# Gate loads moved from SyncE's queue to ScalarE's, value tiles held back, 86 expert tiles ahead instead of 92

## The chip, the cores and the metric

One core of a Trainium2 chip runs the whole program. The metric is the device time of one execution in microseconds; before the change the median of three runs is 1597.53 us (1596.8 to 1598.02). The engines are named as in the profile: PE (matrix multiply), PEld (its weight loads), DVE (vector), ACT (scalar), POOL (GpSimd, which issues the gathers) and SP (SyncE, which here only issues DMAs). ACT issues DMAs too, in line with its own arithmetic.

## The reference

One decoder layer on 512 tokens of width 1024. A first half (a gated mixer, a sparse attention, an output projection) makes h. The second half, where the change lies, adds a product-key expert layer with 16384 one-row experts:

```
q   = rmsnorm(h) @ wq                      # 8 heads, 2 halves of 128
sub = q . subkeys                          # 128 keys a half
pick the 16 best of each half, then the 16 best pairs (i, j) a head
expert = i * 128 + j ;  gate = softmax(best)
a = gelu(x . u_tab[expert]) ;  y = sum gate * a * v_tab[expert]
```

## The kernel before

The first 384 of the 512 tokens take the expert layer densely, the last 128 sparsely by gathering rows.

Dense part. The 16384 experts are 128 tiles of 128 experts. For each tile j, `expert_in(j)` loads the tile of `u_tab` (512 KB, `load_w`, tile `wraw`, three buffers), splits it into a rounded high part (`whi`, ACT, L89) and a low part (`wlo`, DVE, L90), multiplies it with the 384 tokens in 24 matmuls (`pa` in PSUM, two buffers) and takes the result out through a gelu on ACT. Tiles 0 to 39 stay in SBUF. Tiles from 40 up to `AHEAD` are written out by ACT's queue: gelu into `actd` (two buffers, L669) and the spill store `ad<-actd` (L670). These tiles "run ahead": they need no gates. Tiles from `AHEAD` on are made later.

Gates. While the tiles run ahead, the routing code picks experts, and one-hot matmuls (`pg`, L865) build a dense gate matrix. ACT copies it from PSUM into `ch` (L867) and stores it to DRAM as 24 chunks of 1 MB (`gd<-ch`, L869). The numbering here is "1st" to "24th" chunk.

Last stage. For each tile j from 0 to 127: `load_v` loads a value tile (`vraw`, 512 KB, four buffers, split like an expert tile), `load_g` loads the gates of eight tiles at once (`gg`, 1.5 MB in pieces of 512 bytes, two buffers, L904; the first of them in two parts, since chunk 24 is made last), the product of activation, gate and its split (`pr`, `ph`, `pl`) are formed, and 18 matmuls add to `y`. Here the remaining expert tiles and the reads of spilled tiles (`st<-ad`, L921) are mixed in. The sparse part (gathers by POOL, `gt`, dot products and sums on DVE) runs beside all of it.

What sets the order. A scheduler places the instructions of each engine when the program is built; each engine then runs its list strictly in that order. An instruction that waits holds everything behind it on its engine, DMA issues included. The expert loads, value loads, gate loads and reads of spilled tiles are all in SP's list. `tc.issue_after(x)` tells the scheduler to place what it covers behind x. The names used below: expert tile 68 ends in `pa_8208`, 69 in `pa_8242`, 70 in `pa_8279`, 71 in `pa_8313`, 72 in `pa_8350`, 73 in `pa_8384`, 74 in `pa_8421`, 75 in `pa_8455`, 76 in `pa_8492`.

## Time and profile before

| what | value |
|---|---|
| median of three runs | 1597.53 us (1596.8 to 1598.02) |
| the profiled execution, its own time | 1590.94 us |
| its span (first to last instruction) | 1589.2 us |
| PE busy | 1550.9 us, 98% |
| DVE busy | 1265.7 us, 80% |
| ACT busy | 656.9 us, 41% |
| moved by DMA | 387.13 MB, mean 244 GB/s |

The span is first to last instruction; the rest of the execution's time is 1.7 us. PE is "busy" nearly throughout, so time can only come from the places where it is not: the 40 slices of the page show one, slices 21 and 22 (795 to 874 us), where the PE row drops to 6 and 8 while DMA reads 9 and 9. That is the place where the tiles that run ahead meet the start of the last stage. From there to the end DMA is at 8 or 9 of ten in nearly every slice.

### The profile page before, as it was taken

The numbers are of one execution on the slowest core, as the hardware profiler recorded it, in microseconds if no ns is written. First come the engines' busy times: TensorE is split into PE (matmuls) and PEld (weight loads), VectorE is DVE, ScalarE is ACT, GpSimd is POOL, SyncE is SP. The second block draws the span as 40 slices with busy tenths as digits, with TensorE's granted clock in tenths as the row PEclk, the third lists the DMA queues.
The fourth block names the chain that finished last, engine by engine and source line by source line (L and its number), as shares of the span: only waits on it lengthen the run. The fifth ranks groups of instructions, "written<-read, shape, count | busy, mean of one in ns | idle before, by whom it ended". The sixth has DMA issues, their size and how long they took to land.

```text
span 1589.2 us, 22526 instructions
## 1 busy us (share of the span) xinstructions
PE 1550.9 (98%) x8173; PEld 1354.3 (85%) x8173; DVE 1265.7 (80%) x2648; ACT 656.9 (41%) x976; POOL 359.8 (23%) x280
## 2 busy tenths in 40 slices
PE   8998999999999999999968999999999999999998
PEld 6777777888899999999968988888888888888887
DVE  5599945557999999999846688778888878887885
ACT  5453453322335456676713333333333333333332
POOL 0010000000001251111223343333333334344330
PEclk9999999999999999999989999999999999999999
DMA  6211225253213255899899999999999999999983
GB/s 219 80 53 67 93 71 194 93 224 134 80 67 129 84 199 189 294 326 325 318 342 330 349 329 339 340 339 346 347 344 339 347 337 339 337 328 318 323 319 113
DMA packets 154655, 387.13 MB, mean 244 GB/s; under 512 B 12336, under 2 KB 74800, under 8 KB 150960
## 3 DMA queue, kind: packets, MB, share of 16 engines
q1 hardware_dynamic: 106736, 216.07, 38.4%
q0 software_dynamic: 36864, 134.23, 23.8%
q10 hardware_dynamic: 10944, 35.39, 6.0%
q8 instruction: 64, 1.05, 0.3%
q14 instruction: 47, 0.39, 0.1%
HBM read 346.59 MB, written 39.06 MB: 243 GB/s over the span
## 4 chain that ended last, share of the span: by engine, by line
PE 75%; issue 9%; DVE 7%; DMA 7%; POOL 2%; ACT 1%; SPq 0%; POOLq 0%; DVEq 0%; ACTq 0%
PE y L95 9%; PE y L96 9%; PE y L94 9%; PE pa L94 6%; PE pa L95 6%; PE pa L96 6%; DMA gt<-in_v_rows,eid 4%; PE pcol L95 2%; PE pcol L94 2%; PE pcol L96 2%; POOL gt L678 2%; PE pq L94 2%; PE pq L95 2%; PE pq L96 2%; DVE wlo L90 2%
## 5 line engine op out<-in xcount | busy, mean ns | idle before, releaser
L94 PE MATMUL pa<-hh,whi 128*128 128x384 f32 (+2 forms) x1040 | 351.4, 338 | 18.6 <-ACT actd L669 17.7
L95 PE MATMUL pa<-hl,whi 128*128 128x384 f32 (+2 forms) x1040 | 350.7, 337 | 0.0
L96 PE MATMUL pa<-hh,wlo 128*128 128x384 f32 (+2 forms) x1040 | 350.7, 337 | 0.0
L678 POOL DMA_INDIRECT gt<-in_u_rows,eid x128 | 184.4, 1440 | 596.1 <-DVE dots L691 407.3
L95 PE MATMUL y<-wlo,ph 128*128 128x512 f32 x768 | 299.6, 390 | 2.9 <-DVE wlo L90 2.9
L96 PE MATMUL y<-whi,pl 128*128 128x512 f32 x768 | 299.5, 390 | 0.0
L94 PE MATMUL y<-whi,ph 128*128 128x512 f32 x768 | 298.1, 389 | 0.0
L89 ACT CAST whi<-wraw 128x1024 fp32r<-128x1024 f32 x179 | 188.1, 1053 | 243.6 <-PE pa L95 94.4
L90 DVE TENSOR_TENSOR wlo<-wraw,whi 128x1024 fp32r<-128x1024 f32 x179 | 218.2, 1221 | 81.5 <-ACT whi L89 79.4
L678 POOL DMA_INDIRECT gt<-in_v_rows,eid x128 | 163.1, 1274 | 259.7 <-DVE h2l L701 215.8
L94 PEld LDWEIGHTS pa<-hh,whi 128*128 128x128 f32 x1040 | 196.7, 189 | 21.4 <-ACT actd L669 18.6
L934 ACT CAST ph<-pr 128x384 fp32r<-128x384 f32 x128 | 66.0, 516 | 332.4 <-PE y L95 292.6
L95 PEld LDWEIGHTS pa<-hl,whi 128*128 128x128 f32 x1040 | 196.8, 189 | 1.5
L96 PEld LDWEIGHTS pa<-hh,wlo 128*128 128x128 f32 x1040 | 196.6, 189 | 0.4 <-DVE wlo L90 0.4
L701 DVE SCALAR_TENSOR_TENSOR h2l<-gt,coef,h2l 128x1024 f32<-128x1024 f32 x128 | 163.9, 1281 | 36.1 <-DMA gt<-in_v_rows,eid 35.6
L89 ACT CAST whi<-vraw 128x1024 fp32r<-128x1024 f32 x128 | 134.3, 1049 | 107.3 <-PE pa L95 55.2
L691 DVE CUSTOM_DVE_ANT_0 gt<-gt,hn 128x1024 f32<-128x1024 f32 x128 | 155.6, 1220 | 27.1 <-DMA gt<-in_u_rows,eid 25.5
L95 PEld LDWEIGHTS y<-wlo,ph 128*128 128x128 f32 x768 | 144.1, 188 | 33.1 <-DVE wlo L90 3.7
L90 DVE TENSOR_TENSOR wlo<-vraw,whi 128x1024 fp32r<-128x1024 f32 x128 | 156.2, 1220 | 18.1 <-ACT whi L89 17.3
L96 PEld LDWEIGHTS y<-whi,pl 128*128 128x128 f32 x768 | 144.1, 188 | 29.9
L94 PEld LDWEIGHTS y<-whi,ph 128*128 128x128 f32 x768 | 144.2, 188 | 29.1
L867 ACT ACTIVATE ch<-pg 128x512 f32<-128x512 f32 x96 | 97.0, 1108 | 52.5 <-PE pg L865 47.9
(307 smaller groups left out, 2105.9 us busy)
## 6 DMA issues: line engine op xcount, KB each, us to landing
vraw<-in_v_rows SPq DMA_DIRECT2D x128, 512.0 KB
wraw<-in_ut SPq DMA_DIRECT2D x115, 512.0 KB
gd<-ch ACTq DMA_DIRECT2D x24, 1024.0 KB
gg<-gd SPq DMA_DIRECT2D x15, 1536.0 KB
wraw<-in_wcol SPq DMA_DIRECT2D x20, 512.0 KB
ad<-actd ACTq DMA_DIRECT2D x52, 192.0 KB
st<-ad SPq DMA_DIRECT2D x52, 192.0 KB
wraw<-in_wq SPq DMA_DIRECT2D x16, 512.0 KB
```

The source lines that it names most:

```text
L89: A.copy(hi, raw)
L90: V.tensor_tensor(lo, raw, hi.bitcast(F32), ALU.subtract)
L94: T.matmul(ps, lh, rh, start=start, stop=False)
L95: T.matmul(ps, lh, rl, start=False, stop=False)
L96: return T.matmul(ps, ll, rh, start=False, stop=stop)
L678: G.indirect_dma_start(out=t, out_offset=None, in_=table, in_offset=bass.IndirectOffsetOnAxis(ap=eid[:, s:s + 1], axis=0))
L691: V.tensor_tensor_reduce(out=t, in0=t, in1=hn3, scale=1.0, scalar=0.0, op0=ALU.mult, op1=ALU.add, accum_out=dots[:, s:s + 1])
L701: V.scalar_tensor_tensor(h2l, t, coef[:, s:s + 1], h2l, ALU.mult, ALU.add)
L867: A.activation(ch[:, :, to + t4:to + t4 + 4].rearrange("p i t -> p t i"), pg, AF.Copy, scale=1.0 / GS)
L934: A.copy(ph, pr)
```

## The change

`load_g` issues the gate loads on ACT's queue in place of SP's. The gate loads inside the loop are placed behind the last `ph` copy made so far (`hi_copy`) in place of the value load of tile j. `load_w` keeps its load instructions in a list, and value tiles from the third on are placed behind the load of the last expert tile that runs ahead. `AHEAD` is 86, so six expert tiles (86 to 91) move into the last stage, with six spill stores and six reads fewer.

```
--- before.py
+++ after.py
@@ -78,9 +78,11 @@
     TK = 12
     NW = 8
 
+    loads = []
+
     def load_w(src, wp=wp, raws=RAW):
         raw = wp.tile([P, D], F32, name="wraw", tag="wraw", bufs=raws)
-        SY.dma_start(raw, src)
+        loads.append(SY.dma_start(raw, src))
         return split_w(raw, wp)
 
     def split_w(raw, wp=wp):
@@ -636,7 +638,7 @@
     TO = 8
     NCH = ND // TC
     JG = 8
-    AHEAD = 92
+    AHEAD = 86
     KEPT = 40
     EARLY = 2
     GS = 2.0 ** 15
@@ -654,7 +656,7 @@
     stash = ctx.enter_context(tc.tile_pool(name="stash", bufs=1, reuse_waits="tile"))
     big = [stash.tile([P, 3, ND], F32, name=f"st{i}") for i in range((KEPT - 1) // 3)]
     free = [t[:, a, :] for t in big for a in range(3)]
-    pre = {}
+    pre, uload = {}, [None] * len(acts)
     for i, t in enumerate(big):
         pre[len(acts) + 3 * i] = t.rearrange("p a t -> p (a t)")[:, :D]
         SY.dma_start(pre[len(acts) + 3 * i], ut[len(acts) + 3 * i])
@@ -662,6 +664,7 @@
     def expert_in(j):
 
         hi, lo = split_w(pre[j]) if j in pre else load_w(ut[j])
+        uload.append(loads[-1])
         ps = psa.tile([P, S], F32, name="pa", tag="pa")
         expert_mm(ps, hi, lo, 0, ND)
         if KEPT <= j < AHEAD:
@@ -894,14 +897,16 @@
         def load_v(n):
             while len(vq) < min(n, P):
                 raw = wv.tile([P, D], F32, name="vraw")
-                vload.append(SY.dma_start(raw, vt[len(vq)]))
+
+                with tc.issue_after(uload[AHEAD - 1].ins) if len(vq) >= 2 else nullcontext():
+                    vload.append(SY.dma_start(raw, vt[len(vq)]))
                 vq.append(split_w(raw))
 
         def load_g(i):
 
             t = gr[i % 2].tile([P, NCH, JG, TC], F32, name="gg", tag="gg")
             for c0, c1 in ((0, NCH - 1), (NCH - 1, NCH)) if i == 0 else ((0, NCH),):
-                SY.dma_start(t[:, c0:c1], gd[:, c0:c1, i * JG:(i + 1) * JG, :])
+                A.dma_start(t[:, c0:c1], gd[:, c0:c1, i * JG:(i + 1) * JG, :])
             return t
 
         gts = [load_g(0)]
@@ -921,7 +926,7 @@
                 SY.dma_start(acts[j], ad[j - KEPT])
             load_v(j + 1)
             if j % JG == 2 and j + JG < P:
-                with tc.issue_after(vload[j].ins):
+                with tc.issue_after(hi_copy.ins):
                     gts.append(load_g(j // JG + 1))
             hi, lo = vq[j]
             pr = cp.tile([P, ND], F32, name="pr", bufs=2)
@@ -931,7 +936,7 @@
                 free.append(acts[j])
             ph = cp.tile([P, ND], F32R, name="ph")
             pl = cp.tile([P, ND], F32R, name="pl")
-            A.copy(ph, pr)
+            hi_copy = A.copy(ph, pr)
             V.tensor_tensor(pl, pr, ph.bitcast(F32), ALU.subtract)
             for b in range(NB - 1):
                 bs = slice(b * P, (b + 1) * P)
```

What follows shows the built order. `DMAHW3_49` and the like are semaphores of DMA landings, `PE_49`, `DVE_49`, `Activation_49` those of the engines; numbers after a name tell buffers apart.

First place: ACT's list where the last gate chunks are copied out and stored, before the change.

```order
L670 DMA ad_3149<-actd_8196 128x384 [waits Activation_49]
L867 ACTIVATE ch_7645<-pg_7753 128x4x128 [waits PE_49]
L867 ACTIVATE ch_7645<-pg_7763 128x4x128 [waits PE_49]
L89 CAST whi_8309<-wraw_8307 128x1024 [waits DMAHW1_49,DVE_49,PE_49]
L669 ACTIVATE actd_8233<-pa_8208 128x384 [waits DMAHW2_49,PE_49]
L869 DMA gd_3137<-ch_7645 128x2048 [waits Activation_49]
L670 DMA ad_3149<-actd_8233 128x384 [waits Activation_49]
L89 CAST whi_8346<-wraw_8344 128x1024 [waits DMAHW4_49,DVE_49,PE_49]
L669 ACTIVATE actd_8267<-pa_8242 128x384 [waits DMAHW5_49,PE_49]
```

The same place after the change.

```order
L673 DMA ad_3149<-actd_8196 128x384 [waits Activation_49]
L909 DMA gg_8869<-gd_3137 128x23x128 [waits DMAHW3_49]
L870 ACTIVATE ch_7645<-pg_7753 128x4x128 [waits PE_49]
L870 ACTIVATE ch_7645<-pg_7763 128x4x128 [waits PE_49]
L91 CAST whi_8309<-wraw_8307 128x1024 [waits DMAHW1_49,DVE_49,PE_49]
L672 ACTIVATE actd_8233<-pa_8208 128x384 [waits DMAHW2_49,PE_49]
L872 DMA gd_3137<-ch_7645 128x2048 [waits Activation_49]
L673 DMA ad_3149<-actd_8233 128x384 [waits Activation_49]
L91 CAST whi_8346<-wraw_8344 128x1024 [waits DMAHW4_49,DVE_49,PE_49]
L672 ACTIVATE actd_8267<-pa_8242 128x384 [waits DMAHW5_49,PE_49]
```

The first part of the gate load (`gg_8869`, 23 chunks) now stands in ACT's list ahead of the last two gate copies and of the store of chunk 24 (`gd_3137<-ch_7645`); it waits for `DMAHW3`, which is the landing of chunk 23's store (`ch_7516`).

Second place: ACT's list a little later, after the change, with the second part of the first gate load.

```order
L91 CAST whi_8380<-wraw_8378 128x1024 [waits DMAHW7_49,PE_49]
L909 DMA gg_8869<-gd_3137 128x128 [waits DMAHW6_49,DMAHW0_49]
L672 ACTIVATE actd_8304<-pa_8279 128x384 [waits DMAHW1_49,PE_49]
L673 DMA ad_3149<-actd_8304 128x384 [waits Activation_49]
L91 CAST whi_8417<-wraw_8415 128x1024 [waits DMAHW2_49,PE_49]
L672 ACTIVATE actd_8338<-pa_8313 128x384 [waits DMAHW3_49,PE_49]
```

Before, this gate load was absent here and the rest stood in the same order. It waits for `DMAHW0` (the landing of chunk 24) and `DMAHW6` (that of the first part), and the takeout of tile 70 (`actd_8304<-pa_8279`) stands behind it. Ten rows on in ACT's list stands the second gate load, after the change.

```order
L909 DMA gg_8947<-gd_3137 128x24x128
L672 ACTIVATE actd_8375<-pa_8350 128x384 [waits DMAHW1_49]
L939 CAST ph_8951<-pr_8949 128x384 [waits DVE_49]
L673 DMA ad_3149<-actd_8375 128x384 [waits DMAHW6_49,Activation_49]
L672 ACTIVATE actd_8409<-pa_8384 128x384 [waits DMAHW3_49,PE_49]
L673 DMA ad_3149<-actd_8409 128x384 [waits DMAHW0_49,Activation_49]
L91 CAST whi_8522<-wraw_8520 128x1024 [waits DMAHW2_49,PE_49]
```

Behind the second gate load (`gg_8947`, 24 chunks) comes the spill store of tile 72, and behind that the takeout of tile 73.

Third place: SP's list at the same time, before the change.

```order
L83 DMA wraw_8344<-in_ut 128x1024 [waits DMAHW4_49,DVE_49]
L904 DMA gg_9082<-gd_3137 128x23x128 [waits DMAHW3_49,DMAHW6_49,DMAHW2_49,DMAHW7_49,DMAHW0_49,PE_49]
L83 DMA wraw_8378<-in_ut 128x1024 [waits DVE_49]
L83 DMA wraw_8415<-in_ut 128x1024 [waits DMAHW2_49,DMAHW1_49,DVE_49]
L83 DMA wraw_8449<-in_ut 128x1024 [waits DMAHW4_49,DVE_49]
L83 DMA wraw_8486<-in_ut 128x1024 [waits DMAHW7_49,DMAHW5_49,DVE_49]
L904 DMA gg_9082<-gd_3137 128x128 [waits DMAHW6_49,DMAHW0_49]
L897 DMA vraw_9085<-in_v_rows 128x1024
L897 DMA vraw_9091<-in_v_rows 128x1024
L897 DMA vraw_9156<-in_v_rows 128x1024 [waits DMAHW1_49]
L904 DMA gg_9162<-gd_3137 128x24x128 [waits DMAHW2_49,PE_49]
L897 DMA vraw_9191<-in_v_rows 128x1024 [waits DMAHW3_49]
```

And after it.

```order
L85 DMA wraw_8344<-in_ut 128x1024 [waits DMAHW4_49,DVE_49]
L85 DMA wraw_8378<-in_ut 128x1024 [waits DMAHW7_49,DMAHW6_49,DVE_49]
L85 DMA wraw_8415<-in_ut 128x1024 [waits DMAHW2_49,DMAHW1_49,DVE_49]
L85 DMA wraw_8449<-in_ut 128x1024 [waits DMAHW4_49,DVE_49]
L85 DMA wraw_8486<-in_ut 128x1024 [waits DMAHW7_49,DMAHW5_49,DVE_49]
L902 DMA vraw_8872<-in_v_rows 128x1024 [waits PE_49]
L902 DMA vraw_8878<-in_v_rows 128x1024 [waits DMAHW3_49,DMAHW0_49]
L85 DMA wraw_8520<-in_ut 128x1024 [waits DMAHW2_49,DVE_49]
L85 DMA wraw_8557<-in_ut 128x1024 [waits DMAHW4_49,DVE_49]
```

The three gate loads and the third and fourth value tile are gone from between the expert loads; the first two value tiles stay, and the second of them waits for `DMAHW0` (chunk 24). The third value tile now follows the load of tile 85.

## Rows read from the trace of the kernel before

**Rows 1.** The page, part 1: busy time, share, instructions of each engine.

```profile
PE 1550.9 (98%) x8173; PEld 1354.3 (85%) x8173; DVE 1265.7 (80%) x2648; ACT 656.9 (41%) x976; POOL 359.8 (23%) x280
```

**Rows 2.** Windows: us; busy PE, PEld, DVE, ACT, POOL; PE clock; DMA; GB/s.

```profile
784.00:794.00 10.00, 10.00 (x74) 9.69 (x73) 6.17 (x10) 6.52 (x9) 3.56 (x3) 1.00 0.98 333
...
804.00:814.00 10.00, 3.46 (x11) 3.46 (x12) 3.31 (x4) 2.87 (x4) 0.94 (x1) 0.52 0.72 245
...
844.00:854.00 10.00, 10.00 (x60) 10.00 (x59) 5.62 (x9) 4.15 (x6) 3.92 (x4) 1.00 0.96 340
```

**Rows 3.** Timeline of PE: start us, length us, instruction, idle before and releaser.

```profile
801.40 0.34 PE L96 MATMUL pa<-hh,wlo 128*128 128x384 f32 x1
810.54 0.69 PE L94 MATMUL pa<-hh,whi 128*128 128x384 f32 x1 [8.80 <-ACT actd L669]
811.03 0.52 PE L95 MATMUL pa<-hl,whi 128*128 128x384 f32 x1
...
815.14 0.33 PE L94 MATMUL pa<-hh,whi 128*128 128x384 f32 x1
...
820.69 0.34 PE L96 MATMUL pa<-hh,wlo 128*128 128x384 f32 x1
822.78 0.45 PE L94 MATMUL pa<-hh,whi 128*128 128x384 f32 x1 [1.76 <-ACT actd L669]
...
838.52 0.69 PE L94 MATMUL pa<-hh,whi 128*128 128x384 f32 x1 [7.12 <-ACT actd L669]
```

**Rows 4.** Timeline of ACT (ACTq: a DMA issue in its list).

```profile
782.82 0.33 ACTq L869 DMA_DIRECT2D gd<-ch  x1
...
785.61 0.33 ACTq L670 DMA_DIRECT2D ad<-actd  x1
788.47 1.98 ACT L867 ACTIVATE ch<-pg 128x512 f32<-128x512 f32 x2 [1.89 <-PE pg L865]
790.25 1.06 ACT L89 CAST whi<-wraw 128x1024 fp32r<-128x1024 f32 x1
790.48 0.33 ACTq L869 DMA_DIRECT2D gd<-ch  x1
791.20 0.49 ACT L669 ACTIVATE actd<-pa 128x384 f32<-128x384 f32 x1
...
794.75 0.33 ACTq L670 DMA_DIRECT2D ad<-actd  x1
...
809.05 1.04 ACT L89 CAST whi<-wraw 128x1024 fp32r<-128x1024 f32 x1 [10.75 <-DMA wraw<-in_ut]
```

**Rows 5.** SP's DMA issues, from several stretches; a long issue is held.

```profile
792.37 0.38 SPq L904 DMA_DIRECT2D gg<-gd  x1
792.80 9.89 SPq L83 DMA_DIRECT2D wraw<-in_ut  x1
...
813.80 0.61 SPq L904 DMA_DIRECT2D gg<-gd  x1
814.45 12.91 SPq L897 DMA_DIRECT2D vraw<-in_v_rows  x1
...
1314.19 0.53 SPq L904 DMA_DIRECT2D gg<-gd  x1
1317.81 2.81 SPq L83 DMA_DIRECT2D wraw<-in_ut  x1
```

**Rows 6.** Waits of SP, 730 to 900 us: total us, times, longest.

```profile
SPq L904 <- DMA gd<-ch: 9.9, 1, 9.9
```

**Rows 7.** Timeline of ACT: a spill store and the takeout that needs its buffer.

```profile
815.93 0.33 ACTq L670 DMA_DIRECT2D ad<-actd  x1
...
824.16 0.49 ACT L669 ACTIVATE actd<-pa 128x384 f32<-128x384 f32 x1 [1.42 <-DMA ad<-actd]
```

**Rows 8.** Timeline of PE, the last stage: its two gaps.

```profile
1472.14 0.50 PE L95 MATMUL y<-wlo,ph 128*128 128x512 f32 x1 [1.43 <-DVE wlo L90]
...
1539.93 0.50 PE L95 MATMUL y<-wlo,ph 128*128 128x512 f32 x1 [1.49 <-DVE wlo L90]
```

More of the change, by code (lines that the diff above doesn't have):

```diff
@@ L79 @@
     NW = 8
+    loads = []
     def load_w(src, wp=wp, raws=RAW):
         raw = wp.tile([P, D], F32, name="wraw", tag="wraw", bufs=raws)
-        SY.dma_start(raw, src)
+        loads.append(SY.dma_start(raw, src))
         return split_w(raw, wp)
@@ L638 @@
     JG = 8
-    AHEAD = 92
+    AHEAD = 86
     KEPT = 40
@@ L656 @@
     free = [t[:, a, :] for t in big for a in range(3)]
-    pre = {}
+    pre, uload = {}, [None] * len(acts)
     for i, t in enumerate(big):
@@ L664, in expert_in @@
         hi, lo = split_w(pre[j]) if j in pre else load_w(ut[j])
+        uload.append(loads[-1])
         ps = psa.tile([P, S], F32, name="pa", tag="pa")
@@ L896, in load_v @@
                 raw = wv.tile([P, D], F32, name="vraw")
-                vload.append(SY.dma_start(raw, vt[len(vq)]))
+                with tc.issue_after(uload[AHEAD - 1].ins) if len(vq) >= 2 else nullcontext():
+                    vload.append(SY.dma_start(raw, vt[len(vq)]))
                 vq.append(split_w(raw))
@@ L903, in load_g @@
             for c0, c1 in ((0, NCH - 1), (NCH - 1, NCH)) if i == 0 else ((0, NCH),):
-                SY.dma_start(t[:, c0:c1], gd[:, c0:c1, i * JG:(i + 1) * JG, :])
+                A.dma_start(t[:, c0:c1], gd[:, c0:c1, i * JG:(i + 1) * JG, :])
             return t
@@ L923 @@
             if j % JG == 2 and j + JG < P:
-                with tc.issue_after(vload[j].ins):
+                with tc.issue_after(hi_copy.ins):
                     gts.append(load_g(j // JG + 1))
@@ L933 @@
             pl = cp.tile([P, ND], F32R, name="pl")
-            A.copy(ph, pr)
+            hi_copy = A.copy(ph, pr)
             V.tensor_tensor(pl, pr, ph.bitcast(F32), ALU.subtract)
```

## The prediction

> **What bounds the kernel now.** I read the page's busy times first: PE is busy 98% of the span and no other engine is near that [rows 1]. So the change can only win where PE stands, or lose by making it stand elsewhere. The windows show the one place in the part that the change touches: 10.00 of 10 us up to 794, 3.46 in 804 to 814, 10.00 again from 844 [rows 2]. PE's timeline gives the three gaps: 8.80, 1.76 and 7.12 us, each ended by a takeout of a result on ACT (L669) [rows 3]; sum 17.7. After the two long gaps the clock fell: the granted clock was 0.52 in 804 to 814 [rows 2], that is the 1.2 GHz level for much of it, and matmuls at 811.03 take 0.52 us where they take 0.33 at 815.14 [rows 3]. Twelve of them are slow after a long gap; they start 0.32 us apart, against (820.69 - 815.14) / 32 = 0.173 [rows 3]. So 12 x 0.147 = 1.8 us a time, 3.5 for two. The place costs 17.7 + 3.5 = 21.2 us now. An expert tile is 24 matmuls, 24 x 0.173 = 4.17 us, so tile 71 ended its issue at 801.6, 70 at 797.4, 69 at 793.2 (counted back from 801.40 [rows 3]).
>
> Why PE stands: ACT's timeline shows that the takeout stands behind a cast that waited 10.75 us for an expert load [rows 4]. That load was late because of SP: the first gate load waited 9.9 us for the store of chunk 23 [rows 6] and went out at 792.37, and the expert load behind it was held for 9.89 us in its own issue; after the second gate load the next issue was held for 12.91 us [rows 5].
>
> **What goes.** Those holds leave SP's list. The next expert load can go as soon as its buffer is free, which it was while SP stood; it need not wait for 802.69 (792.80 + 9.89). So no cast waits for an expert load any more, and the 21.2 us in their present form go.
>
> **What comes.** The same two waits now stand in ACT's list. I follow ACT by the durations of its rows. An issue behind a gate load on one queue was held until 10.3 us after the gate load's start (792.80 + 9.89 - 792.37), 13.6 us with value loads in front of it, and 6.4 us at 1314.19, the shortest I cite [rows 5]. No row shows a gate load on ACT's queue. In the hold at 792.80, ACT issued a store in 0.33 us at 794.75 [rows 4], so the hold belongs to one queue, and I let ACT's have it: 9.5 us, near the first row but without the store that moved at the same time there. Both ends (0 if ACT's queue does not hold, 13.6) are kept for the range.
>
> Step 1. ACT reaches the first gate load at 785.9 and stands until chunk 23 has landed, 792.2, 9.4 us after its store at 782.82 [rows 4, 6]. It goes on at 792.8: two gate copies 2.0, cast 1.0, takeout of tile 68 0.5, ended 796.3 in place of 791.7 [rows 4]. Tile 70 needs that PSUM buffer: it starts at 796.3, not 793.2. PE stands 3.1 us.
>
> Step 2. The store of chunk 24 is the next issue on ACT's queue: held to 792.4 + 9.5 = 801.9. Then its spill store, cast and takeout of tile 69, 804.1. Tile 70 ended at 800.5, tile 71 starts at 804.2: 3.7 us, and ends at 808.4.
>
> Step 3. The second gate part waits for chunk 24: 801.9 + 9.4 = 811.3; issue 0.4, takeout of tile 70 0.5: tile 72 starts at 812.2 after 3.8 us. Tile 73 follows at once and ends at 820.6.
>
> Step 4. The cast of tile 76 needs tile 73's buffer, so it runs at 820.6 to 821.6, then one `ph` copy, and the second gate load goes out at 822.1. Takeout of tile 72 at 823.2: tile 74 starts after 2.7 us and ends at 827.5.
>
> Step 5. The spill store behind it is held to 822.1 + 9.5 = 831.6, the takeout of tile 73 ends at 832.4: tile 75 starts after 5.0 us, ends at 836.7. The takeout of tile 74 waits for the landing of that spill store (two `actd` buffers). A store of 815.93 freed its buffer only at 824.1, 8.2 us later [rows 7]; so 839.8, and tile 76 starts after 3.2 us and ends at 844.1.
>
> Sum of the gaps: 3.1 + 3.7 + 3.8 + 2.7 + 5.0 + 3.2 = 21.5 us. The clock: gaps of 7.1 and 8.8 us dropped it, one of 1.76 did not [rows 3]; gaps of 3 to 5 lie between. A slow start within steps 1 to 3 is hidden, since there ACT waits for DMAs and PE waits again. I count one of those behind, 1.8 us. The place then costs 23.3 us against 21.2: 2.1 us lost. (Bounds by the hold: each microsecond more or less costs about 2, one through steps 2 to 4 and one through step 5.)
>
> **The rest.** SP's holds behind the fourteen later gate loads go too, and ACT has no DMA behind them in the last stage, so there is no new hold there. In that stage PE stands twice, 1.43 and 1.49 us, each for a DVE split [rows 8]. With six spill stores and six reads fewer, and six expert tiles (25 us of PE) more to spread the transfers over, I let 2 of these 2.9 us go; the bounds are 2.9 gained and 2 lost. PE's work itself is unchanged: the six tiles cost 4.17 us each wherever they stand. The first two value tiles wait for chunk 24 in SP's list, and the expert loads behind them go out at about 813; the first is needed by PE after 844. The third value tile goes out behind tile 85's load, and PE then has some five expert tiles (20 us) to do before it: cost nothing. If a load took over 20 us there, the excess would be paid.
>
> Sum: +2.1 - 2.0 = +0.1 us on the profiled execution's 1590.94 us. The median of the runs is 6.6 us above that execution, and the difference is carried over: 1597.6 us.
>
> **A rule against the gain.** The expert load held for 9.89 us [rows 5] shows that an issue here is not cheap. The Trainium skill says otherwise (DMA: Bandwidth & Descriptors, section "Issuing engines are not separate DMA queues"): all queues end in the same 16 DMA engines, and issuing from several engines saves only the time to initiate a transfer, usually small. By that rule moving the gate loads gains nothing and costs nothing; the rows on hand speak against the "usually small", since the hold is thirty times the 0.33 us of a plain issue. By the rule the time would be that of rival C, by the rows it is the sum above.
>
> **Rivals.** Rival A, faster: ACT's queue does not hold its next issue, or only briefly. For it: ACT's own large stores never held anything (0.33 us each [rows 4]). Against: the stores are few large pieces, gates are 512-byte pieces, and behind these SP was held every time. Without holds step 1 stays at 3.1, step 2 is 0, the landing of chunk 24 behind the gates makes about 3.3 in step 3, step 4 stays near 2.7, and step 5 is 0: 9.1, and one slow start 1.8, so 10.9 against 21.2; with 2 from the last stage 12.3 us less: 1585. It is faster than 0.2% once the hold is under about 8 us.
>
> Rival B, slower: ACT's queue holds longer, because SP's expert and value loads now run beside the gates and share the DMA engines, which were at 333 GB/s already [rows 2]. Its place is steps 2 and 5, its price 2 us per microsecond of hold: with the 13.6 us of the second row [rows 5], 4.1 x 2 = 8.2 us, so 1606. It decides from a hold of 11 us on (1.6 x 2 = 3.2 us). Against: the store of chunk 24, which moved beside the gates before, is now behind them.
>
> Rival C, nothing moves: the transfers are the same and the DMA engines are full (333 to 340 GB/s around the place [rows 2]), so the same bytes take the same time whichever queue issues them, and PE stands as long as before: 1597.5, within 2 us. For it: the loads of the last stage keep DMA at that rate too. Against: PE stood only here, and because of order.
>
> **How the numbers follow.** The forecast (the stall moves from SP to ACT and costs about as much) has 0.42, its own range is a hold of 8 to 11.5 us and one or two slow starts, 1592 to 1602. Rival A 0.30, B 0.22, C 0.06. A difference of 0.2%, 3.2 us, is what a measurement of this kernel can tell from none. The forecast gives 0.10 to faster, 0.27 to no change, 0.05 to slower; A is faster, B slower, C no change: faster 0.40, no change 0.33, slower 0.27. The predicted time is the forecast's, 1597.6. The range takes in A's and most of B's: 1582 to 1607. Below it would be a place that closes altogether (21.2 + 2.9 gone: 1573), above it holds of 14 us with a slow clock after each.
>
> **What would show it.** Right: in the profile after, the ACT list's store of chunk 24 and one spill store have issues of 5 us or more; PE has five or six gaps of 2 to 6 us between 793 and 845, each ended by a takeout, and none of 8; no cast waits over 2 us for an expert load; SP has no issue over 2 us. Tile 76 ends within 3 us of its end now (838.52 + 12 x 0.32 + 12 x 0.173 = 844.4). Wrong: all ACT issues at 0.33 us (A), issues of over 11 us on ACT (B), or PE gaps in the last stage that were not there, which none of my terms holds. If ACT does not stand before the first gate load at all, step 1 is wrong.

## The result and the profile after

The changed kernel is slower by 0.9%: median 1612.76 us (1602.0 to 1616.93, 7 runs) against 1596.8 (1592.09 to 1599.75, 7 runs) of the kernel before, ratio 1.0088, 95% interval 1.0065 to 1.0112. The prediction was 1597.6 us with a range of 1582 to 1607; the measured time lies above it. The profiled execution took 1616.93 us, the longest of the seven, so it shows more of the loss than the median has.

Line numbers after are 2 to 5 higher than before (L669 is L672, L90 is L92, L904 is L909, L869 is L872). The busy times answer to [rows 1]: PE is busy 11.3 us longer in all with the same count of matmuls, so that is slow clock and not work.

```profile
PE 1562.2 (97%) x8173; PEld 1362.2 (84%) x8173; DVE 1264.4 (78%) x2648; ACT 658.8 (41%) x976; POOL 350.8 (22%) x280
```

Two windows split the program at the end of the place that the prediction was about. The columns are those of [rows 2]. First the kernel before, then the changed one:

```profile
780.00:870.00 90.00, 72.32 (x423) 70.64 (x422) 52.10 (x76) 29.73 (x42) 28.16 (x23) 0.91 0.95 334
870.00:1560.00 690.00, 687.04 (x3267) 598.23 (x3266) 565.64 (x702) 243.92 (x339) 254.64 (x205) 1.00 0.94 335
```

```profile
780.00:870.00 90.00, 74.98 (x428) 72.23 (x428) 51.94 (x74) 30.51 (x43) 24.83 (x21) 0.92 0.94 326
870.00:1560.00 690.00, 668.95 (x3150) 581.82 (x3149) 546.95 (x686) 237.46 (x328) 245.31 (x203) 0.99 0.93 326
```

At the transition PE stands 90 - 74.98 = 15.0 us, before 17.7, and the mean granted clock is 0.92, before 0.91: nothing was lost there. In the last stage it stands 690 - 668.95 = 21.0 us, before 3.0. Those 18 us, and the slow clock after each long gap, are nearly all of the loss.

The transition, PE's gaps of the changed kernel (they answer to [rows 3]):

```profile
797.78 0.44 PE L96 MATMUL pa<-hh,whi 128*128 128x384 f32 x1 [2.26 <-ACT actd L672]
803.27 0.44 PE L96 MATMUL pa<-hh,whi 128*128 128x384 f32 x1 [1.03 <-ACT actd L672]
814.05 0.69 PE L96 MATMUL pa<-hh,whi 128*128 128x384 f32 x1 [6.34 <-ACT actd L672]
825.77 0.44 PE L96 MATMUL pa<-hh,whi 128*128 128x384 f32 x1 [1.76 <-ACT actd L672]
839.81 0.45 PE L96 MATMUL pa<-hh,whi 128*128 128x384 f32 x1 [3.63 <-ACT actd L672]
```

And ACT's list there, which answers to [rows 4, 5, 6]:

```profile
794.16 0.38 ACTq L909 DMA_DIRECT2D gg<-gd  x1
794.59 1.90 ACT L870 ACTIVATE ch<-pg 128x512 f32<-128x512 f32 x2 [5.91 <-DMA gd<-ch]
796.52 4.66 ACTq L872 DMA_DIRECT2D gd<-ch  x1
...
801.22 0.44 ACTq L673 DMA_DIRECT2D ad<-actd  x1
...
813.51 0.49 ACT L672 ACTIVATE actd<-pa 128x384 f32<-128x384 f32 x1 [7.09 <-DMA ad<-actd]
...
823.87 0.60 ACTq L909 DMA_DIRECT2D gg<-gd  x1
825.74 5.36 ACTq L673 DMA_DIRECT2D ad<-actd  x1
831.20 0.49 ACT L672 ACTIVATE actd<-pa 128x384 f32<-128x384 f32 x1 [5.09 <-issue]
```

The stall did move from SP's list to ACT's. ACT stood 5.91 us for chunk 23; the store of chunk 24 was held until 7.0 us after the gate load's start (796.52 + 4.66 - 794.16), the spill store behind the second gate load until 7.2 us after (825.74 + 5.36 - 823.87).

The last stage. What PE and DVE waited for between 870 and 1570 us (total us, times, longest), in the kernel before for DVE's gathers:

```profile
DVE h2l L701 <- DMA gt<-in_v_rows,eid: 35.6, 33, 3.1
...
DVE gt L691 <- DMA gt<-in_u_rows,eid: 17.1, 15, 2.5
```

and in the changed kernel for PE and for DVE:

```profile
PE y L97 <- DVE wlo L92: 13.1, 3, 7.7
PE pa L98 <- DVE wlo L92: 8.0, 1, 8.0
```

```profile
DVE h2l L704 <- DMA gt<-in_v_rows,eid: 66.4, 37, 10.0
...
DVE gt L694 <- DMA gt<-in_u_rows,eid: 28.7, 17, 6.1
```

PE's 21.1 us are four waits, each for a low-part split on DVE. DVE's waits for gathered rows went from 52.7 to 95.1 us (the sums of the two lines), and the longest from 3.1 to 10.0.

All four gaps come soon after a later gate load. Three of them, each with the gate load ahead of it (the fourth follows below):

```profile
965.51 0.53 ACTq L909 DMA_DIRECT2D gg<-gd  x1
980.14 0.50 PE L97 MATMUL y<-wlo,ph 128*128 128x512 f32 x1 [1.86 <-DVE wlo L92]
...
1055.63 0.53 ACTq L909 DMA_DIRECT2D gg<-gd  x1
1071.89 0.50 PE L97 MATMUL y<-wlo,ph 128*128 128x512 f32 x1 [3.46 <-DVE wlo L92]
...
1465.85 0.53 ACTq L909 DMA_DIRECT2D gg<-gd  x1
1482.77 0.80 PE L97 MATMUL y<-wlo,ph 128*128 128x512 f32 x1 [7.75 <-DVE wlo L92]
```

PE goes on 14.6, 16.3 and 16.9 us after the gate load was issued, in the gap below 16.7. The other ten of the fourteen later gate loads left no gap of 0.6 us or more in this execution. The fourth gap, followed through ACT, POOL, DVE and PE in the timelines of the changed kernel:

```profile
1415.11 0.53 ACTq L909 DMA_DIRECT2D gg<-gd  x1
...
1414.94 1.86 POOL L681 DMA_INDIRECT gt<-in_v_rows,eid  x1 [2.39 <-DVE h2l L704]
1417.11 0.94 POOL L681 DMA_INDIRECT gt<-in_v_rows,eid  x1 [0.30 <-issue]
1418.64 1.01 POOL L681 DMA_INDIRECT gt<-in_v_rows,eid  x1 [0.59 <-DVE h2l L704]
1430.40 1.01 POOL L681 DMA_INDIRECT gt<-in_v_rows,eid  x1 [10.75 <-DVE h2l L704]
...
1418.29 0.55 DVE L940 TENSOR_TENSOR pl<-pr,ph 128x384 fp32r<-128x384 f32 x1
1428.85 1.28 DVE L704 SCALAR_TENSOR_TENSOR h2l<-gt,coef,h2l 128x1024 f32<-128x1024 f32 x1 [10.01 <-DMA gt<-in_v_rows,eid]
...
1430.52 1.22 DVE L92 TENSOR_TENSOR wlo<-wraw,whi 128x1024 fp32r<-128x1024 f32 x1
...
1431.79 0.69 PE L98 MATMUL pa<-hh,wlo 128*128 128x384 f32 x1 [7.98 <-DVE wlo L92]
```

The gates go out at 1415.11. Three gathers are under way, from 1414.94 on; there are three buffers, so DVE's next sum needs the oldest, and that one comes only at 1428.85, 13.9 us after its issue. Behind the sum in DVE's list stands the split that PE needs. What the queues moved from 1416 to 1420 us (q10 is ACT's, q1 SP's; the gathers' q0 has no line, it moved nothing; columns: packets, MB, share of the 16 engines):

```profile
DMA packets 1478, 0.99 MB, mean 247 GB/s; under 512 B 16, under 2 KB 1411, under 8 KB 1478
...
q10 hardware_dynamic: 1395, 0.71, 64.2%
q1 hardware_dynamic: 83, 0.27, 19.4%
```

In the second half of this stretch, from 1418 to 1420, SP's loads moved nothing either, though a value load had gone out at 1417.16; the gates alone took 82.8%. Such a standstill is not peculiar to ACT's queue. In the kernel before, where a gate load went out on SP's queue at 1359.40, the queues moved this from 1364 to 1366 (nearly all packets are under 2 KB, as pieces of gates are; q1 is SP's, q0 the gathers'):

```profile
DMA packets 1016, 0.55 MB, mean 274 GB/s; under 512 B 2, under 2 KB 1008, under 8 KB 1016
...
q1 hardware_dynamic: 1010, 0.53, 99.6%
q0 software_dynamic: 6, 0.02, 2.6%
```

Yet in that kernel DVE waited for no gather longer than 3.1 us in the whole last stage. So such a standstill alone does not tell the two queues apart; the length of DVE's waits does.

The windows around the gap at 1431.79 show the clock: it was 0.72 in 1424 to 1436 as a mean, the 1.2 GHz level for part of it.

```profile
1424.00:1436.00 12.00, 4.21 (x16) 4.21 (x17) 7.12 (x10) 1.46 (x2) 2.02 (x2) 0.72 0.70 248
```

### The profile page after: what moved, and what is told of

Its sections match the earlier page's. It is cut to its first block, busy times and chain, and to the rows that moved or that the text cites. A ratio compares the mean times of both kernels' runs of the same rounds, so it can differ in the third digit from the quotient of the medians.

```text
span 1615.2 us, 22493 instructions
## 1 busy us (share of the span) xinstructions
PE 1562.2 (97%) x8173; PEld 1362.2 (84%) x8173; DVE 1264.4 (78%) x2648; ACT 658.8 (41%) x976; POOL 350.8 (22%) x280
## 3 DMA queue, kind: packets, MB, share of 16 engines
q10 hardware_dynamic: 59504, 59.38, 11.3%
## 4 chain that ended last, share of the span: by engine, by line
PE 55%; issue 21%; DMA 10%; POOL 7%; DVE 7%; ACT 0%; POOLq 0%; SPq 0%; DVEq 0%; ACTq 0%
DMA gt<-in_v_rows,eid 8%; POOL gt L681 7%; PE y L97 5%; PE y L98 5%; PE y L96 5%; PE pa L96 4%; PE pa L98 4%; PE pa L97 4%; PE pcol L97 2%; PE pcol L96 2%; PE pcol L98 2%; PE pq L96 2%; PE pq L97 2%; PE pq L98 2%; PE pt L96 1%
## 5 line engine op out<-in xcount | busy, mean ns | idle before, releaser
L681 POOL DMA_INDIRECT gt<-in_u_rows,eid x128 | 179.1, 1399 | 613.9 <-DVE dots L694 424.2
L92 DVE TENSOR_TENSOR wlo<-wraw,whi 128x1024 fp32r<-128x1024 f32 x179 | 218.3, 1222 | 81.7 <-ACT whi L91 81.1
L681 POOL DMA_INDIRECT gt<-in_v_rows,eid x128 | 159.5, 1246 | 268.9 <-DVE h2l L704 228.4
L96 PEld LDWEIGHTS pa<-hh,whi 128*128 128x128 f32 x1040 | 197.5, 190 | 19.9 <-ACT actd L672 16.9
L97 PEld LDWEIGHTS y<-wlo,ph 128*128 128x128 f32 x768 | 145.4, 189 | 43.8 <-DVE wlo L92 14.3
L92 DVE TENSOR_TENSOR wlo<-vraw,whi 128x1024 fp32r<-128x1024 f32 x128 | 156.0, 1220 | 17.4 <-ACT whi L91 17.1
```

Source lines behind the costliest of these rows:

```text
L92: V.tensor_tensor(lo, raw, hi.bitcast(F32), ALU.subtract)
L96: T.matmul(ps, lh, rh, start=start, stop=False)
L97: T.matmul(ps, lh, rl, start=False, stop=False)
L681: G.indirect_dma_start(out=t, out_offset=None, in_=table, in_offset=bass.IndirectOffsetOnAxis(ap=eid[:, s:s + 1], axis=0))
```

## The experiments

Each ratio is to runs of the kernel before on the same chip, with its 95% interval. The theories keep their numbers from one expectation to the next; 1 is that the gate loads, as a burst (a whole load of 1.5 MB issued at once) on a queue of their own, make the gathers late. "Idle in the last stage" is 690 us less PE's busy time in the window 870 to 1560 us of one profiled execution: 3.0 before, 21.0 after.

**Which part of the change.** Four runs take it apart.

Gate loads back on SP's queue, all else as changed:

```
-                A.dma_start(t[:, c0:c1], gd[:, c0:c1, i * JG:(i + 1) * JG, :])
+                SY.dma_start(t[:, c0:c1], gd[:, c0:c1, i * JG:(i + 1) * JG, :])
-                with tc.issue_after(hi_copy.ins):
+                with tc.issue_after(vload[j].ins):
```

> The changed kernel with all gate loads back on SP's list (86 tiles ahead and the value tiles behind the last expert tile stay). Theory 1 (gate loads on a queue of their own run beside SP's expert and value loads, the gathers on the third queue come late, DVE waits for them in order, and PE for the DVE split behind): the last stage loses its new gaps, from 28 us of PE excess back to 3 to 8 us; the hold on SP at the transition is back; 1593 to 1600 us. Theory 2 (the loss is from 86 in place of 92 tiles ahead, so six more expert tiles in the last stage): 1608 to 1616, gaps of 3 to 8 us in the last stage stay. Theory 3 (it is from the new place of the value loads): also 1608 to 1616.

Measured: 1594.79 us, ratio 1.0004 (0.9985 to 1.0022), idle 7.6 us.

The queue alone, in the kernel before (92 tiles ahead, value tiles in their old place):

```
-                SY.dma_start(t[:, c0:c1], gd[:, c0:c1, i * JG:(i + 1) * JG, :])
+                A.dma_start(t[:, c0:c1], gd[:, c0:c1, i * JG:(i + 1) * JG, :])
-                with tc.issue_after(vload[j].ins):
+                with tc.issue_after(hi_copy.ins):
```

> The kernel before with one part of the change alone: all gate loads on ACT's queue, each after the high-part copy of the product before; 92 tiles ahead, value tiles where they were. Theory 1 (gates beside the loads starve the gathers): gaps in the last stage of 3 to 8 us each, 15 to 30 us of PE excess there, 1606 to 1618 us. Theory 2 (86 tiles ahead) and theory 3 (place of the value loads): no such gaps, under 6 us of excess in the last stage, 1590 to 1600.

Measured: 1615.52 us, ratio 1.0157 (1.0120 to 1.0193), idle 16.1 us.

86 tiles alone, in the kernel before:

```
-    AHEAD = 92
+    AHEAD = 86
```

> The kernel before with 86 in place of 92 tiles ahead and nothing else. Theory 1: no loss, 1594 to 1600 us. Theory 2: the loss of the changed kernel, 1608 to 1616, with gaps of 3 to 8 us in the last stage where PE waits for a DVE split. Theory 3: no loss.

Measured: 1594.82 us, ratio 1.0003 (0.9988 to 1.0017), idle 6.1 us.

The changed kernel with only the transition's two gate loads on ACT's queue:

```
+                (A if i < 2 else SY).dma_start(t[:, c0:c1], ...)
+                with tc.issue_after((hi_copy if j < JG else vload[j]).ins):
```

> The changed kernel with the first two gate loads (the transition's) on ACT's queue and the other fourteen back on SP's list, each behind the value load it stood behind before. Theory 1: the transition is as in the changed kernel (20 to 23 us of PE excess between 780 and 860), the last stage as before (3 to 8 us); 1592 to 1600 us. Theories 2 and 3: the last stage keeps its gaps, 1608 to 1616.

Measured: 1597.83 us, ratio 1.0026 (1.0006 to 1.0046), idle 7.2 us. So the loss goes with the queue, and most of it with the fourteen later gate loads. The interval of the last run lies just above 1: with the transition's gate loads on ACT's queue it took 3 us more than with all on SP's (1597.83 and 1594.79, same chip). The other two parts cost nothing without the queue (1.0003, 1.0004). With it they seem to ease it: the interval of the queue alone lies above that of the whole change. One caution: a new queue also makes the scheduler build other lists. By the traces, 157 to 211 of DVE's 2648 instructions stand in another place in each of these four than in the kernel that it was made from.

**Bytes, burst or pieces.** The later gate loads in six parts, one a value tile, still on ACT's queue:

```
+            if j > JG and 1 <= j % JG <= 6 and j + JG < P + 7 and j // JG + 1 < P // JG:
+                with tc.issue_after(hi_copy.ins):
+                    load_part(j // JG + 1, j % JG - 1)      # 4 chunks of 24
...
```

> The changed kernel with each of the fourteen later gate loads in six parts of four chunks (512 pieces of 512 bytes), on ACT's queue as there, one part per value tile. The bytes, the pieces, the queue and the loads beside them are the same; only the burst is gone. Theory 1a (a burst of 3072 small pieces on a queue of its own keeps the DMA engines from the gathers, DVE waits for them in order, PE for the DVE split behind): the gaps of 3 to 8 us in the last stage go, PE excess there 3 to 8 us in place of 28; 1588 to 1600 us. Theory 1b (three queues together ask for more bytes than the DMA engines move, burst or not): the gaps stay, smaller and more of them, 15 us or more; 1604 to 1616.

Measured: 1587.03 us, ratio 0.9967 (0.9950 to 0.9983). PE does not stand at all in the last stage, and DVE's waits for gathers are a third:

```profile
870.00:1560.00 690.00, 690.00 (x3279) 601.20 (x3278) 568.54 (x705) 250.54 (x339) 254.03 (x205) 1.00 0.93 330
```

```profile
DVE h2l L704 <- DMA gt<-in_v_rows,eid: 27.6, 31, 2.4
...
DVE gt L694 <- DMA gt<-in_u_rows,eid: 6.6, 9, 1.7
```

The same bytes on the same queue with the same DMA share (0.93 here and after) cost nothing when they are spread. Here too the list is another (160 of DVE's instructions stand elsewhere), so this run alone does not rule out the order.

The later gate loads left out:

```
-                    gts.append(load_g(j // JG + 1))
+                    gts.append(load_g(1) if j < JG else gts[j // JG - 1])
```

> The changed kernel with the fourteen later gate loads left out (each later group of value tiles uses the gates of the first or second group, so that part of the computation is changed); the first two stand where they stood. It gives the price of the later gate loads, whichever way they cost. Theory 1 in both forms: PE excess in the last stage under 4 us, the transition unchanged at 20 to 23; 1585 to 1595 us. If the gathers are late for another reason (the spill reads, six more expert tiles): gaps of 3 us and more stay, 1603 or above.

Measured: 1625.34 us, ratio 1.0201 (1.0173 to 1.0228), idle 26.6 us: a miss for every theory. The scheduler had made another order. With no gate load to wait for, it placed the gathers' work sooner (last column but three: POOL's instructions, 139 in these two windows where the changed kernel has 118), and DVE had 70 short waits for gathers, 3.8 us at most:

```profile
1000.00:1200.00 200.00, 193.77 (x911) 166.34 (x910) 167.63 (x223) 68.47 (x97) 87.28 (x69) 1.00 0.94 331
1200.00:1400.00 200.00, 189.79 (x880) 159.93 (x879) 170.18 (x185) 65.58 (x90) 88.61 (x70) 1.00 0.89 312
```

So another order of DVE's list can cost this much with no gate load at all, and from here on it was a rival of its own (theory 5). Its loss looks different, though: PE's idle time for DVE's splits comes in 30 waits of 2.6 us at most, not in a few long ones behind a gate load.

The same bytes in runs of 12 KB; the engines' lists are row for row those of the changed kernel, but for the shape of the fourteen loads:

```
+            if i > 1:
+                flat = gd.rearrange("p c i t -> p (c i t)")
+                A.dma_start(t..., flat[:, i * NCH * JG * TC:(i + 1) * NCH * JG * TC])
```

> The changed kernel with the fourteen later gate loads reading the same number of bytes in one run of 12 KB per partition in place of 24 pieces of 512 bytes (the gates come in another order, so that part of the computation is changed); queue, place and size are the same. Theory 1a with small pieces as the cause: the landing of a gate load falls from 23 us to under 10, the gaps of the last stage go, 1586 to 1598 us. Theory 1b (bytes, not pieces): the gaps stay, 1604 to 1616.

Measured: 1605.06 us, ratio 1.0076 (1.0052 to 1.0100), idle 14.7 us. Small pieces are at most a small part of it.

To take the order out, the gathers' work was pinned behind each value tile's own subtraction (the kernel places every sum of a gathered row behind `last_v`), and then the bytes of the later gate loads alone were cut:

```
+            last_v = V.tensor_tensor(pl, pr, ph.bitcast(F32), ALU.subtract)
```

> The changed kernel with the gathers' work on DVE pinned: each accumulation of a gathered row stands behind the subtraction of its own value tile in DVE's list, so that the gathers are spread evenly as the program writes them. Gate loads whole, on ACT's queue. It is the base for the next two. Theory 1: the bursts are as they were, gaps of 3 to 8 us stay, 1602 to 1616 us. Theory 5 (the order of DVE's list is the cause): with an even order the gaps go, 1588 to 1598.

Measured: 1604.02 us, ratio 1.0090 (1.0056 to 1.0124). Its runs spread from 1594.79 to 1618.42, and the profiled one was the short end (idle 4.4 us).

```
+            if i > 1:
+                A.dma_start(gts[i - 2][:, 0:1], gd[:, 0:1, i * JG:(i + 1) * JG, :])
+                return gts[i - 2]
```

> The pinned kernel with only one chunk in twenty-four of each of the fourteen later gate loads (64 KB in place of 1536; the other gates stay those of an earlier group, so that part of the computation is changed). The count of DMAs, their queue and their waits are as there, only the bytes are gone. Theory 1: no PE gap over 2 us in the last stage, excess there under 4 us; 1584 to 1594 us. Theory 5: as the pinned kernel within 4 us.

Measured: 1586.02 us, ratio 0.9958 (0.9943 to 0.9973), idle 0.8 us.

```
+                A.dma_start(gts[i - 2][:, 0:16], gd[:, 0:16, i * JG:(i + 1) * JG, :])
```

> As the run before, with sixteen chunks of twenty-four of each later gate load (1024 KB; the rest of the gates stays that of an earlier group). DVE's list is that of the run before but for 17 of 2314 rows. Theory 1: between the two runs before, gaps of 1 to 4 us, PE excess in the last stage 4 to 15 us; 1590 to 1604. Theory 5: as the run before within 3 us, since the order is the same.

Measured: 1591.21 us, ratio 0.9995 (0.9981 to 1.0008), idle 1.7 us. 64 KB, 1024 KB and 1536 KB a gate load give 1586, 1591 and 1604 us. Between the first two the order is all but the same, and theory 5 had them within 3 us, so the 5 us are the bytes'. Theory 1 had expected more idle time there, 4 to 15 us. The last 13 us come with a list of their own (164 of DVE's instructions stand elsewhere), and no run shows how much of them is bytes and how much is order. Theory 5 as the only cause falls; as a part it does not.

The six parts issued together:

```
+                    for k in range(6 if j > 2 else 0):
+                        load_part(j // JG + 1, k)
```

> The changed kernel with each of the fourteen later gate loads split into the six parts of the spread run, but all six issued together where the one load stood; DVE's list is that of the changed kernel but for 61 of 2314 rows. If the burst is the cause: gathers take 8 to 9 us during it as before, gaps of 3 to 8 us stay, 1604 to 1616 us. If it was the single long DMA, or the order that the split run got by chance: 1585 to 1597 as there.

Measured: 1602.01 us, ratio 1.0051 (1.0029 to 1.0073), idle 7.9 us: between the two expectations, and its interval overlaps that of the whole change. The parts were not quite together: behind the first ones the issues were held, so that six took 5 to 12 us, and ACT's own casts stood behind them. One group, with the cast behind it:

```profile
963.43 0.37 ACTq L916 DMA_DIRECT2D gg<-gd  x1
...
963.92 10.68 ACTq L916 DMA_DIRECT2D gg<-gd  x5
974.70 0.51 ACT L948 CAST ph<-pr 128x384 fp32r<-128x384 f32 x1 [9.75 <-DMA gg<-gd]
```

**Is it SP's loads beside the burst?** On SP's queue the loads behind a gate load are held until 6 to 14 us after its start [rows 5]; with the gates on ACT's queue SP can go on issuing. Three runs made SP stand while the gates moved.

```
+            if j > JG and j % JG == 5 and j // JG + 1 < P // JG:
+                with tc.issue_after(vload[j].ins):
+                    SY.dma_start(scr[j // JG], gts[-1][0:1, NCH - 1, 0, :])
```

> The changed kernel with one more DMA of 64 bytes on SP's list for each later gate load: three value tiles after the gate load, SP reads a row of the gates just loaded, so it stands until they have landed, and its expert and value loads stay away from the burst. The lists of PE, DVE, ACT and POOL are those of the changed kernel, row for row, so the order of work is ruled out as a cause of any difference. Theory 1 (the burst runs beside SP's loads and the gathers get what is left): the landing of a gate load falls from 23 us to 10 to 15, DVE's longest wait for a gather from 10 us to under 5, PE excess in the last stage from 28 us to under 8; 1590 to 1600 us. Theory 5 (the order of DVE's list, gathers and splits, is what differs between the kernels): no change, 1605 to 1616.

Measured: 1611.5 us, ratio 1.0117 (1.0093 to 1.0141), idle 18.2 us. Theory 1 as I had it failed here, though SP had sent up to three value loads, with expert loads and spill reads between them, into the burst before it stood. With the gates two value tiles earlier, with and without such a hold:

```
-            if j % JG == 2 and j + JG < P:
+            if j == 2 or j and j % JG == 0 and j + JG < P:
...
+            if j > JG and j % JG == 3 and j // JG + 1 < P // JG:      # held only
```

> The changed kernel with the later gate loads two value tiles earlier on ACT's queue, and one DMA of 64 bytes on SP's list, after the third value load of each group, that reads a row of the gates on their way: SP stands from about the issue of the gates until they have landed, so its expert and value loads do not run beside them. Theory 1 (the burst beside SP's loads leaves the gathers too little): gate loads land in 10 to 15 us, DVE's longest wait for a gather is under 5 us, PE excess in the last stage under 10 us; 1592 to 1600 us. Theory 6 (the moment of issue matters, not SP's loads): the same time as the next run, within 3 us. Theory 7 (a burst of gates on ACT's queue starves the gathers by itself, whatever SP does): gaps of 3 to 8 us stay, 1605 to 1616.

> The same without the DMA that holds SP: the later gate loads two value tiles earlier on ACT's queue, nothing else; the lists of PE, DVE, ACT and POOL are row for row those of the run before. Theory 1: as the changed kernel, gate loads land in 17 to 25 us, gaps of 3 to 8 us, 1604 to 1616 us. Theory 6: 1592 to 1600, gaps under 2 us. Theory 7: 1605 to 1616, as with SP held.

Measured: held 1612.26 us, ratio 1.0110 (1.0068 to 1.0153); not held 1608.89, ratio 1.0074 (1.0046 to 1.0102). The moment of issue is not it, and the hold gave nothing. But it came late again: at one burst (gates at 1399.79) SP sent loads at 1403.94 and 1411.87. So the read was put ahead of those loads:

```
+            if j > JG and j % JG == 1 and j // JG + 1 < P // JG:
+                hold = SY.dma_start(scr[j // JG], gts[-1][0:1, NCH - 1, 0, :])
...
+        with held():                     # issue_after(hold) for every later load
```

> The changed kernel with the later gate loads two value tiles earlier on ACT's queue (as in the two runs before), and SP standing from its third value load of each group on until the gates have landed: the 64-byte read of the gates stands ahead of that load in SP's list, and every expert and value load written behind it stays behind it. Theory 1 (the burst beside SP's loads): SP's loads move under 40 GB/s from 8 to 12 us after the gate load's issue in place of 126 to 138, the gate load's last packet comes by 14 us, DVE's wait for gathers falls from 80 us to under 50, PE excess in the last stage under 10 us; 1592 to 1601 us. Theory 7 (a burst on ACT's queue starves the gathers by itself): gaps of 3 to 8 us on gathers stay, 1605 to 1616. If PE then waits for a value or expert load that came late, the hold was too long and the run tells only of that.

Measured: 1617.04 us, ratio 1.0160 (1.0116 to 1.0205), idle 16.6 us. Now SP did stand (gates at 1404.05, SP's next load at 1419.08), DVE's waits for gathers stayed at 68.5 + 32.3 us, and ACT's casts waited 23.1 us for value loads, as feared in its expectation. In this burst SP's queue had 3.5% of the DMA engines from 1404 to 1419, DVE still waited 2.78 us for a gather, and PE stood 1.29 us for the split behind it, 14.4 us after the gates. That the gathers stay late even then speaks for theory 7, but the hold cost time of its own, and spill reads were not under it.

**Side by side.** Whole later gate loads stand on SP's queue in four of these kernels, each with a list of its own for DVE (the kernel before, gates put back, 86 tiles alone, only the later gates put back): ratios 1, 1.0004, 1.0003 and 1.0026, and DVE's waits for gathers in the last stage are 53 to 80 us. They stand on ACT's queue in eight, with five different lists: ratios 1.0074 to 1.0160, waits 83 to 101 us. The order alone would have to fall the same way by chance each time. And the gaps move with the gates: in the run with the gates two value tiles earlier and SP not held, PE's four gaps over 1 us within 20 us of a gate load end 14.0 to 16.1 us after it, as in the changed kernel. On SP's queue such gaps come too, but shorter: with the gate loads back there, three of 0.8 to 2.5 us end 11.7 to 14.3 us after one.

**Versions.** All gate loads in parts on SP's queue, at the transition behind the loads of expert tiles 75, 77, ... 85; and the same on ACT's queue behind those tiles' casts, the later parts there one value tile earlier and behind `hi_copy`. In both, the first two value tiles go behind tile 82's load:

```
+        for k in range(6):
+            with tc.issue_after(uload[AHEAD - 11 + 2 * k].ins):     # ucast on ACT's queue
+                load_part(0, k)
...
+            if 2 <= j % JG <= 7 and j // JG + 1 < P // JG:
+                with tc.issue_after(vload[j].ins):
+                    load_part(j // JG + 1, j % JG - 2)
```

> The changed kernel with every gate load in six parts of 512 pieces on SP's list: those of the first group behind the loads of expert tiles 75, 77, ... 85, the later ones one behind each value load; the first two value tiles behind tile 82's load. So SP neither waits for the last chunks ahead of an expert load nor is held for long. If holds and waits of long gate loads are the whole cost on either queue: the transition loses its gaps, 21 us of PE excess there fall under 4, the last stage has 3 to 8; 1572 to 1584 us. If small pieces cost the same spread out: 1592 or above.

> The changed kernel with every gate load in six parts on ACT's queue: those of the first group behind the casts of expert tiles 75, 77, ... 85, the later ones one per value tile; the first two value tiles behind tile 82's load. It is the run with all parts on SP's list, on the other queue. If bursts and their holds are the whole cost and the queue is not: no PE gap over 2 us at the transition or in the last stage, 1570 to 1580 us. If ACT's queue costs by itself: gaps in the last stage, 1585 or above.

Measured: on SP's queue 1573.27 us, ratio 0.9881 (0.9852 to 0.9909), the fastest and as expected; on ACT's 1580.75, ratio 0.9919 (0.9893 to 0.9946), just above its expectation. The first one's windows:

```profile
780.00:870.00 90.00, 83.40 (x482) 80.33 (x481) 57.75 (x83) 33.35 (x48) 29.39 (x24) 1.00 0.99 360
870.00:1560.00 690.00, 690.00 (x3272) 600.26 (x3271) 566.75 (x700) 245.01 (x339) 235.31 (x204) 1.00 0.93 327
```

In the last stage PE does not stand at all on either queue. On SP's the clock stays at 2.4 GHz through the transition, where PE stands 6.6 us in place of 17.7; on ACT's the mean clock there is 0.96 and PE stands 8.7 us, with one gap of 3.5. These two runs change the queue, the spreading and the place of the first value tiles together.

## Why the prediction was wrong, point by point

- What bounds the kernel, and that the stall at the transition would move from SP's list to ACT's and cost about the same: right. I had forecast 23.3 us there in place of 21.2; PE stood 15.0 in place of 17.7, at about the same mean clock, so it cost somewhat less and not 2 us more.
- Its steps, forecast and measured: step 1 3.1 and 2.26; step 2 3.7 and 1.03; step 3 3.8 and 6.34; step 4 2.7 and 1.76; step 5 5.0 + 3.2 and 3.63 (its first gap did not come). The hold was 7.0 and 7.2 us, not 9.5, which shortened steps 2 and 5. Step 3 came out longer by another wait than the one I named: the takeout of tile 70 waited for its `actd` buffer, that is for the spill store of tile 68. That store went out at 801.22, behind the held store of chunk 24, and freed the buffer only at 813.5, 12.3 us later. I had counted such a wait in step 5 and left it out here. (An expert tile is 24 x 0.173 = 4.15 us, not 4.17; this changes nothing.)
- "The rest": the step that failed. I wrote that SP's holds behind the fourteen later gate loads go, that ACT has no DMA behind them, and let 2 us be gained, with 2 lost as the bound. No new hold came, as said. But I priced the gates' move only by what stands behind them in a list, not by what else uses the DMA engines at that moment. The gathers do, DVE takes them in order, and the splits for PE stand behind them: 18 us of idle PE and its slow clock in the profiled execution, some 16 us in the medians. No row of the kernel before showed that this term would grow with the other queue.
- Rival B had half of it: that SP's loads "now run beside the gates and share the DMA engines". I put its price into holds at the transition, which grew shorter instead. The runs that held SP did not restore the time, so sharing with SP's loads is not shown to be the cause. What the trace shows is late gathers behind the bursts.
- Rival A had its condition met in part: the holds of 7.0 and 7.2 us are under the 8 that it wanted, and PE stood 2.7 us less at the transition. The gain did not reach the total, since the last stage lost more; that ACT's queue holds nothing (issues of 4.66 and 5.36 us) is out. Rival C (nothing moves) is out: the queue alone made 1.0157. The Trainium skill's rule that I set beside C (DMA: Bandwidth & Descriptors, section "Issuing engines are not separate DMA queues") says that DMAs from all engines run on the same 16 DMA engines and interleave. The trace bears out the sharing: from 1416 to 1420 us the gates of ACT's queue took 64.2% of the engines and SP's loads 19.4%. For those 4 us the gathers did not interleave; they moved nothing. That another issuing engine saves only its issue time, which the page calls usually small relative to the DMA itself (my prediction left these last words out), is not the whole of it here: the other queue alone cost 1.6%.
- Among the signs I had listed "PE gaps in the last stage that were not there, which none of my terms holds". That sign came. Of the signs for being right, five gaps ended by takeouts came (1.0 to 6.3 us), and of the two held issues one was over 5 us (5.36; the other 4.66).

What stays open: why SP's queue takes the same burst nearly unharmed, though the gathers come to a standstill beside it as well. Whole gate loads on it leave 3 to 8 us of idle in the last stage, on ACT's 11 to 21 in seven profiled runs of eight (4.4 in the pinned one). Neither the moment of issue nor a hold of SP's loads told it apart. And no two of these kernels differ in the queue while DVE's list stays row for row the same, so it is not ruled out that the order has a share in the size of the loss.

## What to carry to other kernels

A large DMA moved to another queue is not free because nothing stands behind it in that list: ask which other transfers share the DMA engines with it, which engine waits for them in order, and what stands behind them in that engine's list. Splitting such a load and spreading it over the loop paid here: 0.9967 on ACT's queue for the last stage alone, and with the transition 0.9919 on ACT's and 0.9881 on SP's. On ACT's queue that took back more than going back to SP's did (1.0004). When an experiment leaves work out, look at whether the scheduler kept the order; where it did not, pin it and cut only the bytes.

## What was not expected of the hardware

- A gather came 13.9 us after its issue in a burst (1414.94 to 1428.85); for 4 us none of the gathers' packets moved though three were issued, while the DMA engines moved 247 GB/s. On SP's queue a gate load left the gathers 2.6% of the engines for 2 us in the kernel before.
- With nearly the same order, bursts of 1024 KB cost only 5 us more than bursts of 64 KB over the whole kernel. Whole loads of 1536 KB took 13 us more than that, with another order.
- Runs with whole gate loads on ACT's queue spread widely (1602 to 1617, 1594.8 to 1618.4), those with SP's queue somewhat less (1593.4 to 1596.1 with 86 tiles, 1590.7 to 1601.0 with the gates put back, 1588.9 to 1603.0 for 29 runs of the kernel before). In the changed kernel's profile four of fourteen bursts made a gap.
